# Order of the first mixer's projections, and the counting of split weights, in a two-network kernel on one core

## The chip, the cores and the metric

The kernel runs on one NeuronCore of one Trainium2 chip. The core has TensorE (PE; its weight loads are listed apart as PEld), VectorE (DVE), ScalarE (ACT), GpSimd (POOL) and SyncE (SP), each with its own queue, and sixteen DMA engines. SP's queue issues nearly all loads. The metric is the device time of one launch in microseconds (us), the median of several runs.

## The reference

Two two-layer networks are run one after the other on 256 tokens of width 1024, in float32. The first network has a bidirectional gated DeltaNet mixer (with pooling), a short convolution mixer, and an expert-choice feed-forward with 16 experts behind each; the second has an RG-LRU/SSD layer and a stick-breaking attention layer. Only the first network's first mixer is touched. Cut to what matters:

```
proj = h @ w_in                          # for the latent stream and the context stream
q, k, v = silu(dw_conv(proj[qkv]))       # 4 heads of 128; q only for the latent stream
q, k = l2norm(q), l2norm(k)
t_mat = I + strict_lower(k k^T * decay) * beta     # per chunk of 64 tokens
u, wk = solve(t_mat, v * beta), solve(t_mat, k * beta * exp(gam))
for each chunk, forward and backward:    # context chunks first, then latent chunks
    w = u - wk s;  o = (q exp(gam)) s + (q k^T * decay) w;  s = decay_c s + k_dec^T w
y = [rms_norm(o) * silu(z), pooled] @ w_out
```

## The kernel before

Activations are kept feature-major. Weights come from HBM in chunks of 1 MB (128 x 2048 floats). A float32 product is made of three matmuls: each weight is split into a rounded high part `wh` (ScalarE copy, L209) and a rest `wl` (VectorE subtraction, L284), in parts of 128 x 512, and `ws()` (L321) issues high x high, high x low and low x high for each of 8 blocks. `weight()` (L270) hands out the split parts, in the order that was planned, and splits ahead into a ring of HBUFS = 6 buffers (tags h and l).

Chunks go through small rings: ring_a (2 buffers) for the adaLN weights, ring_b (2 buffers) for `ev_ws` (six chunks: K 0 and 1, V 2 and 3, Q 4 and 5; one chunk serves two heads), `ev_ts` (four, for Z) and `ev_out` (four). A load waits in SP's queue until its buffer is free. The expert weights (`wg`, `wu`, `wd`) use a ring of 12 in the memory that the mixer's tiles leave, and later also ring_a and ring_b.

The first mixer is a list of units, `ORDER["mixer0"]` (L35), that is traced in that order; the tile framework's scheduler then fixes each engine's queue when the kernel is built, from its own estimates, with the trace order as priority. So operations of later units do run ahead where the scheduler saw room. On the chip each queue runs in its fixed order. The units:

- K0 to K3, V0 to V3, Q0 to Q3: `project()` (L630). K and V make a context product of 24 matmuls (`qkvc`, PSUM tag b) and then a latent product of 24 (`qkv`, tag ps); Q has the latent one alone. The eviction is a three-tap convolution (`conv3`, L502: one ScalarE and two VectorE operations per half), Tanh, a VectorE product, and for K and V a transposition (`ktT`, tag a).
- G gates, W0 and W1 decay matrices, R0 to R3 `correlate()` (k k^T times decay, L676), with the diagonal blocks copied out by R2 and R3.
- D `diagonal()` (L714): inverts all 32 x 32 diagonal blocks at once on VectorE, 31 steps of a product and a subtraction (L724, L725) between block transposes; it ends with R and RT.
- I0 to I3, four parts each: `inverse()` (L732) builds the 128 x 128 inverses from the blocks by small products in `lv` (tag b).
- P0 to P3, two parts each: `step()` of the scan, forward and backward. C0 and C1 are the q k scores, U adds the shift to the latent stream in place, Z (four parts) are the gate and pooling projections `zp` (tag ps), A0 to A4 the remaining adaLN products (L424, eight chunks each).

PSUM tags have fixed banks: ps 2, ada 1, a 3, b 2. After the mixer come the pooling and the output norm, the product with `ev_out` (`residual()`), and the first expert layer.

Of the kernel before, what the change touches and what calls it, by code (L numbers as in the profile page):

```python
# [7 lines left out]
F32R = mybir.dt.float32r  # L8
# [5 lines left out]
P = 128  # L14
D = 1024
# [4 lines left out]
RING_A = 2  # L20
RING_B = 2
HBUFS = 6
HBUFS1 = 5
# [7 lines left out]
PART = 512  # L31


ORDER = {
# [139 lines left out]
class Kernel:  # L174
# [84 lines left out]

    def plan(self, pool, bufs, parts):  # L260

        self.hpool, self.hbufs, self.parts = pool, bufs, list(parts)

# [6 lines left out]
    def weight(self, key, i, h, ahead=None):  # L270

        k = (key, i, h)
        if k in self.parts:
            assert self.parts.index(k) <= 1
            self.parts = self.parts[self.parts.index(k):]
            for k_ in self.parts[:ahead or self.hbufs]:
                if k_ not in self.WS:
                    hl = [self.more_parts.get(k_, self.hpool).tile([P, PART], F32R, tag=n, name="w" + n) for n in "hl"]
                    self.WS[k_] = self.split(self.W[k_[0]][k_[1]][:, k_[2] * PART:(k_[2] + 1) * PART], *hl)
        return self.WS[k]  # L280
# [237 lines left out]
    def mixer0_parts(self):  # L518
        r = []
        for n in ORDER["mixer0"].split():  # L520
            if n[0] in "KVQ":
                r += self.ws_parts("ev_ws", [4 * "KVQ".index(n[0]) + int(n[1])])
            elif n == "Z":
                j = len([x for x in r if x[0] == "ev_ts"])
                r += self.ts_parts("ev_ts", range(2))[j:j + 4]
        return r

    def mixer0(self, xin, xp):

        nc, v, g = self.nc, self.nc.vector, self.nc.gpsimd  # L530
        tc = self.tc
# [4 lines left out]
        right = ExitStack()  # L536
        self.plan(right.enter_context(tc.tile_pool(name="hpool0", bufs=HBUFS, side="right")), HBUFS, self.mixer0_parts())
        hl_p = right.enter_context(tc.tile_pool(name="m0l", bufs=1, side="right"))
# [89 lines left out]
        rq = kp.tile([P, 2, 4], F32, name="rq")  # L628

        def project(part, h):  # L630

            n = 256 if part == 2 else 512
            segs = []
            if part < 2:
                segs.append(self.ps("qkvc", "b")[:, :256])
                self.ws(segs[0], "ev_ws", 4 * part + h, ctx)
            a = self.ps("qkv")
# [19 lines left out]
            b = self.ps("ktT", "a")  # L657
# [222 lines left out]
        units = {"G": gates, "W0": each(decays(0), 4), "W1": each(decays(1), 4), "U": whole, "D": invert, "C0": lambda: scores(0), "C1": lambda: scores(1), "Z": each(zpool(), 4)}  # L880
        for h in range(4):
            units[f"K{h}"] = lambda h=h: project(0, h)
            units[f"R{h}"] = lambda h=h: cor(h)
            units[f"V{h}"] = lambda h=h: project(1, h)
            units[f"Q{h}"] = lambda h=h: project(2, h)
            units[f"I{h}"] = each(inverse(pairs[h]), 4)
            units[f"P{h}"] = each(steps(h), 2)
# [877 lines left out]
    def second(self):  # L1765
# [8 lines left out]
        with (self.tc.tile_pool(name="hpool2", bufs=HBUFS, side="right") as hpool,  # L1774
# [3 lines left out]
            self.chunks(parts)  # L1778
            self.plan(hpool, HBUFS, [x for x in parts if x[0] != "e_gate"])
            h = pr.tile([P, KT, T2], F32, name="h2")  # L1780
# [122 lines left out]
```

## Time and profile before

| | us |
|---|---|
| median of 3 runs | 1262.93 |
| lowest and highest | 1258.85, 1270.01 |
| profiled execution, its own time | 1264.06 |
| its span in the profile | 1262.3 |

| engine | busy us | share of the span |
|---|---|---|
| PE | 1102.4 | 87% |
| PEld | 752.2 | 60% |
| DVE | 635.5 | 50% |
| ACT | 492.8 | 39% |
| POOL | 68.0 | 5% |

Times in the rows below are from the span's start. Busy time counts the engine's own instructions; the ends of matmuls are modelled. PEclk is the granted TensorE clock as a share of full speed. DMA share is the mean busy share of the sixteen DMA engines. In rows of groups, "x16" is the number of instructions, then come the busy time, the mean length of one in ns, and the idle time in front of them with what ended it. In this kernel a line such as L209, L230 or L284 is that of a helper, and the tile names tell the use. A fp32 matmul on plain float32 data is recorded as two instructions.

### The profile page before, as it was taken

The page shows a single profiled execution, that of the slowest core. Times are in us where ns is not written, and L with a number is a line of the kernel's source. Part 1 is how long each engine was busy: PE and PEld are TensorE (multiplying, and loading weights), DVE is VectorE, ACT ScalarE, POOL GpSimd, SP SyncE. Part 2 cuts the span into 40 slices and gives each one's busy share as a digit, 9 for nine tenths or more (in the row PEclk, how much of TensorE's full clock was granted, in tenths as well). Part 3 has the DMA queues.
Part 4 walks back from the last instruction along what each step waited for, and adds up shares of the span by engine and source line. Part 5 has one row for each costly group of instructions (what it writes and reads, how often), then busy time and mean ns, then how long its engine had stood idle before and what let it go on. Part 6 is the DMA issues. An engine that isn't in the chain of part 4 may idle for free.

```text
span 1262.3 us, 19466 instructions
## 1 busy us (share of the span) xinstructions
PE 1102.4 (87%) x7728; PEld 752.2 (60%) x7728; DVE 635.5 (50%) x1442; ACT 492.8 (39%) x1035; POOL 68.0 (5%) x118
## 2 busy tenths in 40 slices
PE   5999699998799776699979967668999999999997
PEld 2667367767544211189954421116898699988875
DVE  3448854634421100178731110016887888689875
ACT  4346254424211000165521100005788465566663
POOL 0050000000000000000000000000001100011100
PEclk9899689999799867899979987778999999999999
DMA  9578655457999999999459999995252135433220
GB/s 387 198 278 319 235 201 201 138 214 310 401 421 420 421 421 422 422 420 383 167 224 383 421 421 422 421 422 218 102 199 101 67 139 185 165 134 130 101 101 34
DMA packets 48043, 339.71 MB, mean 269 GB/s; under 512 B 5328, under 2 KB 5584, under 8 KB 7248
## 3 DMA queue, kind: packets, MB, share of 16 engines
q1 hardware_dynamic: 46800, 336.38, 67.4%
q10 hardware_dynamic: 1152, 2.09, 0.5%
q8 instruction: 61, 1.00, 0.3%
q14 instruction: 30, 0.25, 0.1%
HBM read 337.40 MB, written 1.05 MB: 268 GB/s over the span
## 4 chain that ended last, share of the span: by engine, by line
PE 54%; DMA 26%; issue 7%; DVE 7%; ACT 4%; POOL 2%; POOLq 0%; SPq 0%; DVEq 0%; ACTq 0%
DMA w<-wu 8%; DMA w<-wd 8%; DMA w<-wg 7%; PE gu L1100 3%; PE ada L424 3%; PE xg L1075 2%; PE qkvg L329 2%; PE qkvg L331 2%; PE sc L329 2%; PE sc L330 2%; PE sc L331 2%; PE qkvg L330 2%; DMA w<-sc_in 1%; PE res L330 1%; PE res L329 1%
## 5 line engine op out<-in xcount | busy, mean ns | idle before, releaser
L284 DVE TENSOR_TENSOR wl<-w,wh 128x512 fp32r<-128x512 f32 x304 | 209.1, 696 | 83.3 <-ACT wh L209 79.2
L209 ACT ACTIVATE wh<-w 128x512 fp32r<-128x512 f32 x304 | 188.8, 629 | 154.5 <-PE res L330 27.2
L1100 PE MATMUL gu<-w,xg 128*32 128x512 f32 x1024 | 158.3, 721 | 46.6 <-DMA w<-wu 27.0
L1100 PEld LDWEIGHTS gu<-w,xg 128*32 128x32 f32 x1024 | 30.7, 118 | 158.1 <-DMA w<-wu 74.0
L1126 PE MATMUL dn<-w,hidT 128*32 128x512 f32 x512 | 74.5, 686 | 21.0 <-DMA w<-wd 15.1
L230 DVE SCALAR_TENSOR_TENSOR xT<-sc,adac,xT 128x256 f32<-128x256 f32 x64 | 27.9, 479 | 111.1 <-PE sc L1134 111.1
L209 ACT ACTIVATE y<-dn 128x512 f32<-128x512 f32 x16 | 9.6, 597 | 189.9 <-PE dn L1126 189.9
L1115 DVE TENSOR_TENSOR hid<-hid,gu 128x512 f32<-128x512 f32 x8 | 5.5, 685 | 153.8 <-PE gu L1100 153.8
L329 PE MATMUL qkvg<-u_f,wh 128*128 128x272 f32 (+1 forms) x256 | 74.3, 290 | 0.0
L331 PE MATMUL qkvg<-u_f,wl 128*128 128x272 f32 (+1 forms) x256 | 73.2, 286 | 0.0
L330 PE MATMUL qkvg<-u_f,wh 128*128 128x272 f32 (+1 forms) x256 | 72.8, 284 | 0.0
L424 PE MATMUL ada<-w,cs 128*32 128x512 f32 x320 | 51.1, 650 | 7.2 <-DMA w<-ada 7.2
L331 PE MATMUL sc<-hT,wl 128*128 128x258 f32 x192 | 54.5, 284 | 0.9 <-DVE wl L284 0.9
L1126 PEld LDWEIGHTS dn<-w,hidT 128*32 128x32 f32 x512 | 14.6, 118 | 68.2 <-DMA w<-wd 38.3
L329 PE MATMUL sc<-hT,wh 128*128 128x258 f32 x192 | 54.7, 285 | 0.2 <-ACT hT L289 0.2
L330 PE MATMUL sc<-hT,wh 128*128 128x258 f32 x192 | 54.3, 283 | 0.0
L329 PEld LDWEIGHTS qkvg<-u_f,wh 128*128 128x128 f32 x256 | 48.2, 188 | 3.1 <-issue 2.0
L331 PEld LDWEIGHTS qkvg<-u_f,wl 128*128 128x128 f32 x256 | 48.3, 189 | 0.8 <-issue 0.8
L330 PEld LDWEIGHTS qkvg<-u_f,wh 128*128 128x128 f32 x256 | 48.2, 188 | 0.0
L1134 PE MATMUL sc<-sg,y 128*128 128x256 f32 x128 | 40.2, 469 | 8.3 <-ACT y L209 8.3
L1134 PEld LDWEIGHTS sc<-sg,y 128*128 128x128 f32 x128 | 28.5, 234 | 26.8 <-ACT y L209 22.3
L1114 ACT ACTIVATE hid<-gu 128x512 f32<-128x512 f32 x8 | 4.8, 597 | 100.5 <-PE gu L1100 100.5
(613 smaller groups left out, 2642.5 us busy)
## 6 DMA issues: line engine op xcount, KB each, us to landing
w<-wu SPq DMA_DIRECT2D x64, 1024.0 KB, 19.8
w<-wg SPq DMA_DIRECT2D x64, 1024.0 KB, 19.8
w<-wd SPq DMA_DIRECT2D x64, 1024.0 KB, 19.8
w<-ada SPq DMA_DIRECT2D x48, 1024.0 KB, 5.0
w<-f_in SPq DMA_DIRECT2D x16, 1024.0 KB, 4.8
w<-sc_in SPq DMA_DIRECT2D x12, 1024.0 KB, 20.7
w<-e_out SPq DMA_DIRECT2D x8, 1024.0 KB, 5.4
w<-ev_ws SPq DMA_DIRECT2D x6, 1024.0 KB, 6.0
```

Of the source, the lines that this page charges most:

```text
L209: return self.nc.scalar.activation(out, in_, AF.Copy)
L230: return self.nc.vector.scalar_tensor_tensor(out, a, s, b, op0=op0, op1=op1, **kw)
L284: self.nc.vector.tensor_sub(lo, x, hi.bitcast(F32))
L329: mm(out, wh, xh, start=(kt == 0), stop=False)
L330: mm(out, wh, xl, start=False, stop=False)
L331: self.last_mm = mm(out, wl, xh, start=False, stop=(kt == nk - 1)).ins
L424: nc.tensor.matmul(a[32 * q:32 * q + 32, :], self.cs[:, kt, :], w[:, q * 512:(q + 1) * 512], start=(kt == 0), stop=(kt == KT - 1), tile_po ...
L1075: nc.tensor.matmul(a[:, :256], xn[:, i, ft * P:(ft + 1) * P], oh[:, i].rearrange("p e s -> p (e s)"), start=(i == 0), stop=(i == 1))
L1100: nc.tensor.matmul(a[32 * e:32 * e + 32, :], xg[g // 2][:, kt, s:s + 32], w[:, e * 512:(e + 1) * 512], start=(kt == 0), stop=(kt == KT - 1 ...
L1115: v.tensor_mul(hid, hid, pu[1])
L1126: nc.tensor.matmul(a[32 * e:32 * e + 32, :], hT[:, t, 32 * e:32 * e + 32], w[:, e * 512:(e + 1) * 512], start=(t == 0), stop=(t == 3), til ...
L1134: nc.tensor.matmul(a[:, j * 256:(j + 1) * 256], y[:, (2 * f2 + j) * P:(2 * f2 + j + 1) * P], sg[g // 2][:, g % 2], start=True, stop=True)
```

## The change

The mixer's order is rewritten: all K, then Q0, R0 to R3, all V (V3 ahead of V2) and Q1 to Q3 stand ahead of D; A2 and A3 stand behind it, U ahead of P0, and C0 and the four parts of each I are placed anew. The context product of K and V becomes a unit of its own (k0 to k3, v0 to v3), which leaves its bank in `first` for project(). The mixer's ring of split parts has 7 buffers instead of 6. `weight()` now counts the uses that each part has left (8 for a K or V part, 4 by default, 1 or 2 for the token-major ones) and splits the next part into a buffer when the part in it has none left, so a part may be asked for again after later ones.

```diff
@@ -19,6 +19,7 @@
 T2 = 272
 RING_A = 2
 RING_B = 2
+HBUFS0 = 7
 HBUFS = 6
 HBUFS1 = 5
 EARLY = 1, 2
@@ -32,8 +33,9 @@
 
 
 ORDER = {
-    "mixer0": "K0 G A0 W0 A1 W1 W0 W1 W1 W1 W0 W0 K1 R0 K2 A2 K3 R1 A3 R2 R3 V0 D V1 I0 V2 I0 V3 I1 Q0 I0 Q1 I0 I1 "
-          "Q2 I1 P0 P0 I3 P1 I1 Q3 C0 U P1 I2 Z I2 C1 P2 Z Z I2 I3 I2 P3 P2 A4 I3 Z I3 P3",
+    "mixer0": "k0 K0 G A0 W0 A1 W1 W0 W1 W1 W1 W0 W0 k1 K1 k2 K2 k3 K3 Q0 R0 R1 R2 R3 v0 V0 v1 V1 v3 V3 v2 V2 Q1 Q2 "
+              "Q3 D A2 A3 I0 I0 I1 I0 I0 I1 U I1 P0 I2 I3 P1 I1 P0 P1 C0 Z I2 C1 P2 Z Z I2 I3 P3 I2 P2 A4 I3 Z I3 "
+              "P3",
     "e": "L0 L1 U L3 L6 L2 L5 L7 L4 X9 X10 G2 G3 G4 G0 G6 G1 G7 X11 G5 X7 X6 X0 X2 X1 X5 X8 X4 Z1 X3 Z7 DT T "
           "Z3 S R Z0 R S S S Z2 R Z4 R H S S M Z6 O5 H Z5 O6 O3 O0 O1 H O7 N0 O2 H O4 N1",
     "f": "J1 J0 J3 J2 J4 B0 J5 J6 J7 B0 B0 B1 J8 J10 J9 B1 J11 B1 B2 J12 J13 J15 B2 J14 B3 B2 J19 J16 J17 B3 "
@@ -257,9 +259,13 @@
         self.nc.sync.dma_start(t, src)
         self.W.setdefault(key, {})[i if i is not None else len(self.W[key])] = t
 
-    def plan(self, pool, bufs, parts):
-
-        self.hpool, self.hbufs, self.parts = pool, bufs, list(parts)
+    def plan(self, pool, bufs, parts, uses=None):
+
+
+        self.hpool, self.hbufs, self.parts, self.nsplit = pool, bufs, list(parts), 0
+        self.left = {k: (uses or {}).get(k, 1 if k[0] in self.TS else 4) for k in self.parts}
+
+    TS = "ev_ts", "f_out"
 
     def ws_parts(self, key, ms, nk=KT):
         return [(key, i // 16, i % 16 // 4) for m in ms for i in range(m * nk, m * nk + nk, 4)]
@@ -270,13 +276,20 @@
     def weight(self, key, i, h, ahead=None):
 
         k = (key, i, h)
-        if k in self.parts:
-            assert self.parts.index(k) <= 1
-            self.parts = self.parts[self.parts.index(k):]
-            for k_ in self.parts[:ahead or self.hbufs]:
-                if k_ not in self.WS:
-                    hl = [self.more_parts.get(k_, self.hpool).tile([P, PART], F32R, tag=n, name="w" + n) for n in "hl"]
-                    self.WS[k_] = self.split(self.W[k_[0]][k_[1]][:, k_[2] * PART:(k_[2] + 1) * PART], *hl)
+        at = self.parts.index(k)
+        while self.nsplit < min(len(self.parts), at + (ahead or self.hbufs)):
+            k_ = self.parts[self.nsplit]
+            pool = self.more_parts.get(k_, self.hpool)
+            if pool is self.hpool:
+                old = [x for x in self.parts[:self.nsplit] if x not in self.more_parts][-self.hbufs:]
+                if len(old) == self.hbufs and self.left[old[0]] > 0:
+                    break
+            hl = [pool.tile([P, PART], F32R, tag=n, name="w" + n) for n in "hl"]
+            self.WS[k_] = self.split(self.W[k_[0]][k_[1]][:, k_[2] * PART:(k_[2] + 1) * PART], *hl)
+            self.nsplit += 1
+        assert at < self.nsplit
+        if ahead is None:
+            self.left[k] -= 1
         return self.WS[k]
 
     def split(self, x, hi, lo, eng="act"):
@@ -518,8 +531,9 @@
     def mixer0_parts(self):
         r = []
         for n in ORDER["mixer0"].split():
-            if n[0] in "KVQ":
-                r += self.ws_parts("ev_ws", [4 * "KVQ".index(n[0]) + int(n[1])])
+            if n[0] in "kvKVQ":
+                p = self.ws_parts("ev_ws", [4 * "KVQ".index(n[0].upper()) + int(n[1])])
+                r += [x for x in p if x not in r]
             elif n == "Z":
                 j = len([x for x in r if x[0] == "ev_ts"])
                 r += self.ts_parts("ev_ts", range(2))[j:j + 4]
@@ -534,7 +548,8 @@
         keep = ExitStack()
         kp = keep.enter_context(tc.tile_pool(name="m0r", bufs=1, side="right"))
         right = ExitStack()
-        self.plan(right.enter_context(tc.tile_pool(name="hpool0", bufs=HBUFS, side="right")), HBUFS, self.mixer0_parts())
+        self.plan(right.enter_context(tc.tile_pool(name="hpool0", bufs=HBUFS0, side="right")), HBUFS0, self.mixer0_parts(),
+                  {k: 8 for k in self.ws_parts("ev_ws", range(8))})
         hl_p = right.enter_context(tc.tile_pool(name="m0l", bufs=1, side="right"))
         rc = ExitStack()
         self.pack_in("pkg", hl_p)
@@ -627,13 +642,18 @@
         rk = pr.tile([P, 4, 4], F32, name="rk")
         rq = kp.tile([P, 2, 4], F32, name="rq")
 
+        first = {}
+
+        def project_ctx(part, h):
+
+            a = self.ps("qkvc", "b")[:, :256]
+            self.ws(a, "ev_ws", 4 * part + h, ctx)
+            first[part, h] = a
+
         def project(part, h):
 
             n = 256 if part == 2 else 512
-            segs = []
-            if part < 2:
-                segs.append(self.ps("qkvc", "b")[:, :256])
-                self.ws(segs[0], "ev_ws", 4 * part + h, ctx)
+            segs = [first.pop((part, h))] if part < 2 else []
             a = self.ps("qkv")
             self.ws(a[:, :258], "ev_ws", 4 * part + h, lat)
             segs.insert(0, a[:, :256])
@@ -879,6 +899,8 @@
 
         units = {"G": gates, "W0": each(decays(0), 4), "W1": each(decays(1), 4), "U": whole, "D": invert, "C0": lambda: scores(0), "C1": lambda: scores(1), "Z": each(zpool(), 4)}
         for h in range(4):
+            units[f"k{h}"] = lambda h=h: project_ctx(0, h)
+            units[f"v{h}"] = lambda h=h: project_ctx(1, h)
             units[f"K{h}"] = lambda h=h: project(0, h)
             units[f"R{h}"] = lambda h=h: cor(h)
             units[f"V{h}"] = lambda h=h: project(1, h)
@@ -1776,7 +1798,7 @@
               self.tc.tile_pool(name="second", bufs=1) as pr):
             up = us.enter_context(self.tc.tile_pool(name="input", bufs=1, side="right"))
             self.chunks(parts)
-            self.plan(hpool, HBUFS, [x for x in parts if x[0] != "e_gate"])
+            self.plan(hpool, HBUFS, [x for x in parts if x[0] != "e_gate"], {k: 2 for k in self.ts_parts("f_out", [1])})
             h = pr.tile([P, KT, T2], F32, name="h2")
             self.layer_e(up, pr, h)
             self.dump("h1", h)
```

## Rows read from the trace of the kernel before

**Rows 1.** Engine time by stretch of the span; the first line names the columns.
```profile
core 0: us, PE busy (x) PEld busy (x) DVE busy (x) ACT busy (x) POOL busy (x), PEclk, DMA share, GB/s
...
99.00:132.70 33.70, 30.64 (x243) 22.60 (x243) 29.33 (x85) 19.62 (x56) 1.14 (x1) 1.00 0.79 282
132.70:148.50 15.80, 5.99 (x33) 0.72 (x33) 14.50 (x36) 1.94 (x6) 0.00 (x0) 0.65 0.90 348
148.50:162.50 14.00, 13.96 (x93) 10.46 (x94) 6.84 (x27) 7.87 (x25) 0.31 (x1) 0.54 0.23 76
162.50:200.00 37.50, 37.50 (x381) 27.41 (x382) 17.43 (x44) 19.40 (x54) 0.61 (x2) 0.95 0.68 244
200.00:277.00 77.00, 77.00 (x589) 55.11 (x586) 39.35 (x107) 31.14 (x82) 0.92 (x3) 1.00 0.48 167
...
345.00:572.00 227.00, 185.25 (x1178) 80.79 (x1178) 51.13 (x117) 37.65 (x71) 1.23 (x1) 0.86 1.01 421
```

**Rows 2.** Loads issued by SyncE's queue, 272 to 306 us: start, length, line, transfer, count.
```profile
272.20 4.28 SPq L257 DMA_DIRECT2D w<-wu  x2
285.51 0.33 SPq L257 DMA_DIRECT2D w<-wg  x1
...
303.67 2.08 SPq L257 DMA_DIRECT2D w<-wg  x4
```

**Rows 3.** Matmuls in order of time, 128 to 150 us; idle before in brackets.
```profile
128.64 0.29 PE L330 MATMUL qkv<-hl,wh 128*128 128x258 f32 x1
128.76 0.28 PE L331 MATMUL qkv<-hl,wl 128*128 128x258 f32 x1
...
132.69 1.06 PE L424 MATMUL ada<-w,cs 128*32 128x512 f32 x8
136.21 1.07 PE L424 MATMUL ada<-w,cs 128*32 128x512 f32 x8 [2.45 <-DMA w<-ada]
...
148.52 0.60 PE L754 MATMUL lv<-RT,A 32*32 32x32 f32 x8 [2.65 <-DVE RT L728]
149.05 0.58 PE L329 MATMUL qkvc<-hc,wh 128*128 128x256 f32 x1
```

**Rows 4.** ScalarE in order of time, 147 us.
```profile
147.13 1.90 ACT L209 ACTIVATE A<-R 32x128 f32<-32x128 f32 x6 [13.81 <-DVE R L727]
```

**Rows 5.** VectorE groups, 111.5 to 148.5 us: line, tiles, count, busy, mean ns, idle.
```profile
L725 DVE TENSOR_TENSOR ident<-ident,sub 128x31 f32<-128x31 f32 (+15 forms) x31 | 10.6, 341 | 0.8
L724 DVE TENSOR_TENSOR sub<-B,ident 128x31 f32<-128x31 f32 (+15 forms) x31 | 10.6, 341 | 0.7
L284 DVE TENSOR_TENSOR wl<-w,wh 128x512 fp32r<-128x512 f32 x6 | 4.1, 687 | 0.2 <-ACT wh L209 0.2
...
L230 DVE SCALAR_TENSOR_TENSOR cv<-sq,cv 128x512 f32<-128x512 f32 x2 | 1.4, 689 | 0.0
```

**Rows 6.** Matmul groups, 148.5 to 277 us.
```profile
L424 PE MATMUL ada<-w,cs 128*32 128x512 f32 x136 | 23.8, 658 | 0.0
...
L329 PE MATMUL qkv<-hl,wh 128*128 128x258 f32 x24 | 7.9, 329 | 0.0
...
L331 PE MATMUL qkvc<-hc,wl 128*128 128x256 f32 x16 | 6.1, 381 | 0.0
...
L653 PE MATMUL qkv<-ones,sq 128*128 128x1 f32 x16 | 2.2, 243 | 0.0
...
L202 PE MATMUL ktT<-ident,cv 128*128 128x128 f32 x8 | 1.7, 353 | 0.0
```

**Rows 7.** VectorE groups, 42 to 290 us.
```profile
L230 DVE SCALAR_TENSOR_TENSOR qT<-qkv,dnh,qT 128x255 f32<-128x255 f32 x8 | 3.8, 480 | 0.2
...
L230 DVE SCALAR_TENSOR_TENSOR lat<-hl,adac,hl 128x256 f32<-128x256 f32 x8 | 3.8, 478 | 0.1
...
L697 DVE TENSOR_TENSOR A<-kb,A 128x256 f32<-128x256 f32 x8 | 3.4, 424 | 0.1
L284 DVE TENSOR_TENSOR hl<-lat,hl 128x256 fp32r<-128x256 f32 x8 | 3.4, 422 | 1.0 <-ACT hl L209 1.0
```

## Prediction

> **What bounds the kernel now.** I read the stretches first. From 345 to 572 us the sixteen DMA engines are full (share 1.01) and TensorE waits on expert weights; in the mixer, 99 to 277 us, it is the other way round, TensorE is busy nearly everywhere and the DMA share is about half [rows 1]. The one hole in the mixer is 132.7 to 148.5 us: TensorE is busy 5.99 of 15.80 us, ScalarE 1.94, VectorE 14.50. The granted clock is 0.65 of full in it and 0.54 in the 14 us behind it, so most of that time lies at the lower of its two levels (1.2 instead of 2.4 GHz), and 0.95 up to 200 us [rows 1].
>
> Next, whether an earlier end of the mixer is worth its full length. SyncE's queue issues the first expert weight that needs the mixer's memory at 285.5 us, and the run of them at 303.7 us, after the last `ev_out` chunk [rows 2]. From there the DMA engines are full for over 200 us. So a microsecond taken from the mixer's end is a microsecond of the kernel, until something else holds those loads (a rival below).
>
> Then what TensorE waits for in the hole. In order of time it has only adaLN chunks, each when its load lands, and the hole ends with the first `lv` product of I0 on RT, the last result of the substitution D; the next matmul is a context product, `qkvc` [rows 3]. That order is the clue. `lv` and `qkvc` share PSUM tag b with two banks; before, I0 is traced ahead of V2, so V2's context product gets its bank behind I0's, and I0 waits for D. V2 and V3 have their latent halves done but can't be evicted, they hold split weights, and Q's eviction stands in ScalarE's queue behind the copy that waits 13.81 us for R [rows 4]. That banks go out in trace order is my reading of these rows, not a row.
>
> **The change part by part.** *Context products as units, and counted uses.* Each small unit stands right ahead of its large one (`v3 V3`), which is the order that project() had; the counting lets a part's buffer go after its last use, as the tile release does now. No instruction is added. I cost both at nothing. The seventh buffer lets a split start half a product earlier, about 12 x 0.12 us, hidden while TensorE has other products; from nothing to that gain.
>
> *V and Q ahead of D and I0.* This takes the wait for the bank away. What comes out of the time after 148.5 us: V2's and V3's context products, 48 matmuls, and three latent ones of Q, 72 matmuls (16 and 24 on each of three lines) [rows 6]. Their spacing at the full clock is 0.12 us [rows 3], so 5.8 + 8.6 us; with the transposes of V2 and V3 and the row sums of Q (busy 1.7 and 2.2 us, overlapping, I take 3) 17.4 us in all. They go into the hole.
>
> The price is on VectorE, which runs D without a pause in the second half of the hole [rows 4, 5]. D is 62 operations, 21.2 us busy [rows 5], and each eviction pushed in delays it by its own length. New ahead of D's end: V2's other half, 2 x 0.48 + 0.69; V3, 4 x 0.48 + 0.69; four Q at 3 x 0.48 (the third is shorter, I have its bound); four weight splits for Q2 and Q3 at 0.69 [rows 5, 7]. That is 1.7 + 2.6 + 5.8 + 2.8 = 12.8 us. R0 to R3 now follow all four K, so that up to three of them bunch ahead of D: between nothing and 3 x 4 x 0.42 = 5.1 us [rows 7], I take half, since R0's and R1's small operations can still run early. Left out of the sum, as it depends on the order that the scheduler picks: U (8 x (0.48 + 0.42) = 7.2 us) and the first seven splits for Z (4.8 us) could be put between D's steps too [rows 5, 7].
>
> So D ends at 148.5 + 12.8 + 2.5 = 163.8 us. From 132.7 us that is 31.1 us, in which TensorE has the 17.4 us and adaLN chunks, one per 3.52 us as they land, 1.07 us each [rows 3]: nine, 9.6 us. Idle: 31.1 - 27.0 = 4.1 us, against 9.8 now.
>
> *A2 and A3 behind D.* Their eight chunks each become the filler of last choice. The four that ran in the hole before and five more are in the sum above; 17 stood after it [rows 6], 12 would now. Ring a has two buffers, so SyncE's queue stands still behind an adaLN load while TensorE puts its chunk off; the ring b loads queued behind it (the `ev_ts` and `ev_out` chunks) then come late for Z. I cost that at nothing, with Z still 50 us away, and keep up to 5.3 us (five chunks not taken forward) for the range.
>
> *Ring b.* Q0 and Q1 share a chunk that now holds one of two buffers from Q0 to Q1, and V3 and V2 load into the other. Their chunk is wanted only after V0 and V1 (four products, 11.5 us at 24 x 0.12 each); I cost it at nothing, with one pace of 3.5 us as the other end.
>
> **The sum.** After D the old stretch is 128.5 us (148.5 to 277). Take away 14.0 x 0.46 + 37.5 x 0.05 = 8.3 us that the lower clock cost [rows 1], the 17.4 us moved and the five chunks moved, 5.3 us: 97.5 us. A hole of 4.1 us instead of 9.8 should leave some of the clock loss, 2 us. The mixer's matmuls end at 163.8 + 97.5 + 2 = 263.3 instead of 277, 13.7 us earlier; I take 13 for the small gaps that less filler leaves. The profiled execution took 1264.06 us (span 1262.3), 1.1 above the median of 1262.93 and inside its runs' 1258.85 to 1270.01: 1251 against itself, 1250 against the median.
>
> **Rivals.**
> 1. *The hole moves.* U and Z's splits do go between D's steps: D ends at 175.8 us, TensorE has 17.4 us and twelve chunks, 12.8 us, for 43.1 us, idle 13, and the clock falls as before. End 175.8 + 97.5 - 3.2 + 8.3 = 278.4: no gain, 1263. For it: VectorE already mixes foreign operations into D (six splits among its 62 steps [rows 5]). Against: the same U lets Z start, which fills. The same time comes out if the last adaLN loads set the end: two ring a buffers come free for expert weights only at 272 us [rows 2].
> 2. *Slower: the chain behind D, not TensorE, sets its length.* I0 to P3 is one chain of hand-offs between TensorE, ScalarE and VectorE. If the old 120.2 us (128.5 less the clock's 8.3) are that chain, taking filler out shortens nothing, and D's delay passes on whole: 163.8 + 120.2 = 284, 7 us late, up to 296 with D at 175.8; with D in the middle 290, 1276. It decides from a chain of 277 - 163.8 = 113 us. For it: four inverses and four scan pairs stand in series with nothing but Z, A4 and U beside them. Against: TensorE is busy 77.00 of 77 us at the end [rows 1], and the matmuls of the chain begin one after the other without idle time.
> The Trainium skill, Perfetto Trace Analysis, section Identifying the Most-Contended Engine, speaks for this rival: matmul busy time says little on how near TensorE is to its limit, weight-load busy time is the measure. By it the last stretch is loaded 55.11 of 77 us, 72%, so 28% would be waits, which less filler doesn't shorten. The trace has no gaps there, but the busy ends are modelled, so it doesn't refute it.
> 3. *The hole closes whole.* The idle 9.8, the clock's 8.3 and the 3.1 idle us of 99 to 132.7 [rows 1] all go: 21 us, 1242. For it: Z's 96 products could join. Against: D's delay.
>
> **How the numbers follow.** Forecast 0.50, with its own range 1242 to 1258; rival 3 0.14; rival 1 0.22; rival 2 0.14. A measurement of this kernel can tell about 1%, 12.6 us, so faster means below 1250.3. That takes a little over half of the forecast's chance (0.28) and rival 3: 0.42. Slower is rival 2, 0.14; the rest, 0.44, lies within 1%. The range goes from rival 3 with the gains left open (the earlier split, R's at nothing, some 4 us) to where rival 2 begins to weigh: 1238 to 1272.
>
> **What would show it.** Right: no idle stretch above 5 us on TensorE between 99 us and D's end; all `qkvc` products before the first `lv`; D's last operation near 164 us; granted clock above 0.9 behind it; the first expert load into the mixer's memory near 272 us instead of 285.5; everything behind moved by the same amount. Wrong: a hole of 10 us or more ahead of the first `lv` (rival 1), or small waits of TensorE on ScalarE and VectorE all through the scan with P3's end at or after 284 us (rival 2), or the expert loads not moved although P3 ends earlier.

## The result and the profile after

| | before | after |
|---|---|---|
| median, us (4 runs of each, same chip) | 1263.04 | 1248.61 |
| lowest and highest, us | 1258.85, 1270.01 | 1247.82, 1252.43 |
| profiled execution, us | 1264.06 | 1252.43 |
| its span, us | 1262.3 | 1250.7 |

The ratio after to before is 0.9884, 95% interval 0.9862 to 0.9906: faster by 14.4 us, with 13 forecast. The profiled execution of after is the slowest of its four, so the two profiles are only 11.6 us apart. Executions more than 1.5% above the fastest of their kernel are left out of the ratios: five of nine with U behind D, two of ten with D ahead of V, no others.

The stretches of the span of after, to be held against [rows 1]; the last two are moved to where the same work now lies:

```profile
core 0: us, PE busy (x) PEld busy (x) DVE busy (x) ACT busy (x) POOL busy (x), PEclk, DMA share, GB/s
99.00:132.70 33.70, 33.42 (x273) 28.18 (x272) 31.22 (x88) 25.64 (x72) 1.14 (x1) 1.00 0.69 248
132.70:148.50 15.80, 14.55 (x108) 11.48 (x106) 14.64 (x42) 10.45 (x25) 0.00 (x0) 1.00 0.60 215
148.50:162.50 14.00, 12.16 (x46) 5.82 (x46) 11.51 (x33) 3.85 (x9) 0.00 (x0) 0.63 0.68 232
162.50:200.00 37.50, 36.16 (x337) 22.75 (x337) 23.29 (x68) 20.07 (x57) 0.92 (x3) 0.95 0.73 273
200.00:265.00 65.00, 65.00 (x555) 42.40 (x549) 20.63 (x65) 19.54 (x63) 0.92 (x3) 1.00 0.52 176
331.00:558.00 227.00, 183.98 (x1156) 77.68 (x1156) 48.71 (x111) 36.38 (x69) 1.24 (x1) 0.86 1.01 418
```

Read the second row first: in the old hole TensorE is busy 14.55 of 15.80 us, where it was 5.99, and the clock is full instead of 0.65. The weight-load column says more than the busy one, 11.48 us against 0.72: these are products, not late adaLN chunks. In the third row a weaker stretch is left (the clock at 0.63), but it lies ahead of D's end and not behind it. The experts' stretch in the last row is what it was: full DMA engines for 227 us, 14 us earlier.

TensorE in order of time, idle before in brackets, against [rows 3]:

```profile
149.11 1.93 PE L437 MATMUL ada<-w,cs 128*32 128x512 f32 x8 [1.32 <-DMA w<-ada]
152.27 1.01 PE L673 MATMUL qkv<-ones,sq 128*128 128x1 f32 x4 [1.22 <-ACT sq L671]
153.21 1.93 PE L437 MATMUL ada<-w,cs 128*32 128x512 f32 x8
155.07 0.80 PE L353 MATMUL zp<-wh,hl 128*128 128x512 f32 x1
...
172.29 1.06 PE L437 MATMUL ada<-w,cs 128*32 128x512 f32 x8
174.54 0.51 PE L353 MATMUL zp<-wh,hl 128*128 128x512 f32 x1 [1.18 <-DVE zp L232]
...
175.88 0.43 PE L774 MATMUL lv<-RT,A 32*32 32x32 f32 x8
```

The longest idle time between 132 us and the first `lv` is 1.32 us. Before, there were four waits in the hole, of 2.45, 4.20, 0.54 and 2.65 us, 9.8 in all; the longest, which [rows 3] leave out, was

```profile
141.47 1.93 PE L424 MATMUL ada<-w,cs 128*32 128x512 f32 x8 [4.20 <-DMA w<-ada]
```

The first `lv` comes at 175.88 us, 27.4 us later than before. What fills is new: from 155.07 us on `zp`, Z's products. By the order of TensorE's queue 51 of the 96 stand ahead of the first `lv`, and none did before; all eight context products of K and V stand ahead of it too.

VectorE at D's end, in order of time:

```profile
169.09 0.24 DVE L745 TENSOR_TENSOR ident<-ident,sub 128x87 f32<-128x87 f32 x1
169.25 0.42 DVE L297 TENSOR_TENSOR hl<-lat,hl 128x256 fp32r<-128x256 f32 x1
169.59 0.22 DVE L744 TENSOR_TENSOR sub<-B,ident 128x60 f32<-128x60 f32 x1
169.72 0.48 DVE L232 SCALAR_TENSOR_TENSOR lat<-hl,adac,hl 128x256 f32<-128x256 f32 x1
170.11 0.22 DVE L745 TENSOR_TENSOR ident<-ident,sub 128x60 f32<-128x60 f32 x1
170.24 0.69 DVE L297 TENSOR_TENSOR wl<-w,wh 128x512 fp32r<-128x512 f32 x1
...
171.99 1.98 DVE L747 STREAM_TRANSPOSE R<-ident 128x1024 f32<-128x1024 f32 x1
173.82 0.67 DVE L232 SCALAR_TENSOR_TENSOR zp<-zp 128x512 f32<-128x512 f32 x1
174.41 1.21 DVE L748 STREAM_TRANSPOSE RT<-R 128x1024 f32<-128x1024 f32 x1
```

Every second operation is foreign to D: U's `lat` and `hl` pairs, and the splits `wl` for Z. RT ends at 175.6 us. ScalarE's copy that waited 13.81 us for R [rows 4] waits no more:

```profile
174.13 1.90 ACT L211 ACTIVATE A<-R 32x128 f32<-32x128 f32 x6
```

SyncE's queue, against [rows 2]: the first `wg` load comes 10.8 us earlier, the run of four 13.4 us.

```profile
266.46 5.15 SPq L259 DMA_DIRECT2D w<-wu  x2
273.59 0.33 SPq L259 DMA_DIRECT2D w<-ev_out  x1
274.69 1.79 SPq L259 DMA_DIRECT2D w<-wg  x4
...
290.30 2.17 SPq L259 DMA_DIRECT2D w<-wg  x4
```

### The profile page after: what moved, and what is told of

Same layout as the page of the kernel before. It is cut to its first block, busy times and chain, and to the rows that moved or that the text cites. A ratio compares the mean times of both kernels' runs of the same rounds, so it can differ in the third digit from the quotient of the medians.

```text
span 1250.7 us, 19471 instructions
## 1 busy us (share of the span) xinstructions
PE 1094.5 (88%) x7728; PEld 741.0 (59%) x7728; DVE 629.2 (50%) x1442; ACT 492.8 (39%) x1035; POOL 68.6 (5%) x118
## 4 chain that ended last, share of the span: by engine, by line
PE 39%; DMA 23%; issue 7%; DVE 5%; ACT 2%; POOL 1%; POOLq 0%; DVEq 0%; SPq 0%; ACTq 0%
DMA w<-wu 8%; DMA w<-wg 8%; DMA w<-wd 6%; PE gu L1122 3%; PE xg L1097 2%; PE sc L344 2%; PE sc L342 2%; PE sc L343 2%; PE qkvg L342 2%; PE qkvg L344 2%; PE qkvg L343 2%; DMA pk<-pk 1%; PE dn L1148 1%; PE res L342 1%; PE res L343 1%
## 5 line engine op out<-in xcount | busy, mean ns | idle before, releaser
L1122 PE MATMUL gu<-w,xg 128*32 128x512 f32 x1024 | 161.0, 729 | 50.9 <-DMA w<-wu 28.1
L1148 PE MATMUL dn<-w,hidT 128*32 128x512 f32 x512 | 70.4, 652 | 21.7 <-DMA w<-wd 16.1
L437 PE MATMUL ada<-w,cs 128*32 128x512 f32 x320 | 54.6, 641 | 1.3 <-DMA w<-ada 1.3
L1156 PE MATMUL sc<-sg,y 128*128 128x256 f32 x128 | 37.3, 442 | 8.5 <-ACT y L211 8.4
```

The lines of the kernel that those rows point to most:

```text
L437: nc.tensor.matmul(a[32 * q:32 * q + 32, :], self.cs[:, kt, :], w[:, q * 512:(q + 1) * 512], start=(kt == 0), stop=(kt == KT - 1), tile_po ...
L1122: nc.tensor.matmul(a[32 * e:32 * e + 32, :], xg[g // 2][:, kt, s:s + 32], w[:, e * 512:(e + 1) * 512], start=(kt == 0), stop=(kt == KT - 1 ...
L1148: nc.tensor.matmul(a[32 * e:32 * e + 32, :], hT[:, t, 32 * e:32 * e + 32], w[:, e * 512:(e + 1) * 512], start=(t == 0), stop=(t == 3), til ...
L1156: nc.tensor.matmul(a[:, j * 256:(j + 1) * 256], y[:, (2 * f2 + j) * P:(2 * f2 + j + 1) * P], sg[g // 2][:, g % 2], start=True, stop=True)
```

## The experiments

Theory 1 is the prediction's: V2's and V3's context products stood behind I0 for a bank of tag b, in trace order; with V ahead, TensorE works while VectorE inverts, and the mixer ends earlier by the TensorE time that is no longer lost. Rivals: it is not the order but the number of banks; it is Q, or the adaLN chunks, or the seventh buffer; the chain of hand-offs behind D sets the end and TensorE's volume does not. Ratios are to the kernel before, run beside each on the same chip.

**V ahead of the first I0, nothing else** (in the kernel before; D, A2, A3, Q and R at their old places):

```diff
-    "mixer0": "K0 G A0 W0 A1 W1 W0 W1 W1 W1 W0 W0 K1 R0 K2 A2 K3 R1 A3 R2 R3 V0 D V1 I0 V2 I0 V3 I1 Q0 I0 Q1 I0 I1 "
+    "mixer0": "K0 G A0 W0 A1 W1 W0 W1 W1 W1 W0 W0 K1 R0 K2 A2 K3 R1 A3 R2 R3 V0 D V1 V2 V3 I0 I0 I1 Q0 I0 Q1 I0 I1 "
```

> Kernel before with one edit: V1, V2 and V3 traced ahead of I0, still behind D; Q, the six buffers, U, A2 and A3 stay where they were. Theory 1 (the two banks of tag b go out in trace order, and I0's product held the bank of V2's context product): the 48 context matmuls run ahead of the first lv product, the hole of 9.8 us shrinks to under 4 us, and at least two thirds of the change's 14 us come: 1248 to 1254 us. Rival (V and Q must stand ahead of D, or the seventh buffer and the counting do it): 1259 to 1266 us.

Measured: 1251.88 us, ratio 0.9905 (0.9873 to 0.9938). Two units, V2 and V3, moved ahead of the first I0 give some 12 of the 14.4 us. D stays ahead of them in the trace, so this is the order of V and I0 alone. In order of time:

```profile
157.83 0.28 PE L331 MATMUL qkv<-hl,wl 128*128 128x258 f32 x1
160.40 0.41 PE L754 MATMUL lv<-RT,A 32*32 32x32 f32 x8 [0.28 <-DVE RT L728]
```

The first line is the last of all the latent products. All 192 context products run ahead of the first `lv` now, and so do Q's 72 latent ones that stood behind it before, though nobody moved Q. TensorE is idle 4.1 us from 132 us to the first `lv`. None of U's operations and none of Z's products come ahead of D's end here, so D is less delayed than in the whole change, and with less to fill.

**The first I0 back ahead of V3 and V2** (in the kernel after; D moves ahead of them with it):

```diff
-    "mixer0": "k0 K0 G A0 W0 A1 W1 W0 W1 W1 W1 W0 W0 k1 K1 k2 K2 k3 K3 Q0 R0 R1 R2 R3 v0 V0 v1 V1 v3 V3 v2 V2 Q1 Q2 "
-              "Q3 D A2 A3 I0 I0 I1 I0 I0 I1 U I1 P0 I2 I3 P1 I1 P0 P1 C0 Z I2 C1 P2 Z Z I2 I3 P3 I2 P2 A4 I3 Z I3 "
+    "mixer0": "k0 K0 G A0 W0 A1 W1 W0 W1 W1 W1 W0 W0 k1 K1 k2 K2 k3 K3 Q0 R0 R1 R2 R3 v0 V0 v1 V1 D I0 v3 V3 v2 V2 Q1 Q2 "
+              "Q3 A2 A3 I0 I1 I0 I0 I1 U I1 P0 I2 I3 P1 I1 P0 P1 C0 Z I2 C1 P2 Z Z I2 I3 P3 I2 P2 A4 I3 Z I3 "
```

> Changed kernel with one edit: D and the first part of I0 traced ahead of V3 and V2, the rest as changed. Theory 1: the context products of V3 and V2 wait for the first lv product again, TensorE is idle 8 us or more ahead of it, and the time goes back to 1257 to 1266 us. Rival (the order of the banks doesn't matter, the rest of the new order brings the gain): 1247 to 1252 us.

Measured: 1256.51 us, ratio 0.9935 (0.9913 to 0.9958), just under what was expected. TensorE in order of time is the picture of [rows 3] again:

```profile
139.47 1.63 PE L437 MATMUL ada<-w,cs 128*32 128x512 f32 x8 [4.16 <-DMA w<-ada]
...
152.86 0.60 PE L774 MATMUL lv<-RT,A 32*32 32x32 f32 x8 [2.04 <-DVE RT L748]
153.39 0.58 PE L342 MATMUL qkvc<-hc,wh 128*128 128x256 f32 x1
```

The context product comes half a microsecond behind the first `lv`, with no wait of its own. Some 7 of the 14.4 us are lost again. The time alone doesn't say to what, since D's move ahead of V costs as much by itself (D ahead of V, below); what I0's place does is seen in the order: with I0 ahead, 48 context products stand behind the first `lv`; with D alone ahead, none.

**Three banks instead of two** (in the kernel before):

```diff
-    BANKS = {"ps": 2, "ada": 1, "a": 3, "b": 2}
+    BANKS = {"ps": 2, "ada": 1, "a": 2, "b": 3}
```

> Kernel before with three banks in tag b and two in tag a, order unchanged. Theory 1 in its strict form (a tag's banks are given out in trace order, so V2's context product stands behind I0's product whatever their number): the context products of V2 and V3 still run behind the first lv product, the hole of 8 to 12 us stays, and the time is 1260 us or more. Rival (two banks are simply too few): all eight context products run ahead of lv and 5 us or more are gained.

Measured: 1267.65 us, ratio 1.0021 (1.0000 to 1.0042). In order of time:

```profile
145.14 1.93 PE L424 MATMUL ada<-w,cs 128*32 128x512 f32 x8 [5.24 <-DMA w<-ada]
150.81 0.60 PE L754 MATMUL lv<-RT,A 32*32 32x32 f32 x8 [3.74 <-DVE RT L728]
151.35 0.58 PE L329 MATMUL qkvc<-hc,wh 128*128 128x256 f32 x1
```

A third bank gains nothing: `lv` still stands ahead of `qkvc`, with the same 48 context products behind it. They run between I0's own products (the next `lv` comes at 153.94 us), so a bank was free for them. The order is the cause, not the number of banks; the price of the bank taken from tag a is in this time too. That it is the order within tag b, the kernel before shows: nine units' latent products (216, in tag ps) ran ahead of its first `lv`, three units more than are traced ahead of I0, and only the context products waited.

**Q1 to Q3 traced behind D again** (in the kernel after):

```diff
-    "mixer0": "k0 K0 G A0 W0 A1 W1 W0 W1 W1 W1 W0 W0 k1 K1 k2 K2 k3 K3 Q0 R0 R1 R2 R3 v0 V0 v1 V1 v3 V3 v2 V2 Q1 Q2 "
-              "Q3 D A2 A3 I0 I0 I1 I0 I0 I1 U I1 P0 I2 I3 P1 I1 P0 P1 C0 Z I2 C1 P2 Z Z I2 I3 P3 I2 P2 A4 I3 Z I3 "
+    "mixer0": "k0 K0 G A0 W0 A1 W1 W0 W1 W1 W1 W0 W0 k1 K1 k2 K2 k3 K3 Q0 R0 R1 R2 R3 v0 V0 v1 V1 v3 V3 v2 V2 "
+              "D A2 A3 I0 I0 I1 Q1 I0 I0 I1 Q2 Q3 U I1 P0 I2 I3 P1 I1 P0 P1 C0 Z I2 C1 P2 Z Z I2 I3 P3 I2 P2 A4 I3 Z I3 "
```

> Changed kernel with Q1 to Q3 traced behind D and among the parts of I0 and I1. Q uses no bank of tag b, so by theory 1 it runs ahead of the first lv product anyway and the time stays within 4 us of the changed kernel's: 1246 to 1253 us. Rival (placing Q ahead of D carries half of the gain): 1254 to 1259 us.

Measured: 1248.90 us, ratio 0.9874 (0.9837 to 0.9910), not to be told from the change. In order of time:

```profile
150.94 0.28 PE L344 MATMUL qkv<-hl,wl 128*128 128x258 f32 x1
167.08 0.43 PE L774 MATMUL lv<-RT,A 32*32 32x32 f32 x8
```

This is again the last latent product: Q uses no bank of tag b, and all of its products run ahead of the first `lv` wherever Q is traced. So Q needed no place ahead of D in the trace; the run doesn't show what Q behind D on the chip would cost. The scheduler did place U anew: three of its `lat` operations lie ahead of D's end instead of eight, 17 of Z's products ahead of the first `lv` instead of 51, and RT ends at 165.8 us.

**Six buffers for the split weights** (in the kernel after, `HBUFS0 = 6`):

> Changed kernel with six buffers for split weights instead of seven. The prediction put the seventh between nothing and 1.4 us: 1247 to 1253 us. Rival (the buffers carry a part of the gain, as the held weights of V2 and V3 filled four of six before): 1255 us or more.

Measured: 1250.83 us, ratio 0.9894 (0.9849 to 0.9940). The seventh buffer cannot be measured.

**A2 and A3 at their old places** (in the kernel after):

```diff
-    "mixer0": "k0 K0 G A0 W0 A1 W1 W0 W1 W1 W1 W0 W0 k1 K1 k2 K2 k3 K3 Q0 R0 R1 R2 R3 v0 V0 v1 V1 v3 V3 v2 V2 Q1 Q2 "
-              "Q3 D A2 A3 I0 I0 I1 I0 I0 I1 U I1 P0 I2 I3 P1 I1 P0 P1 C0 Z I2 C1 P2 Z Z I2 I3 P3 I2 P2 A4 I3 Z I3 "
+    "mixer0": "k0 K0 G A0 W0 A1 W1 W0 W1 W1 W1 W0 W0 k1 K1 k2 K2 A2 k3 K3 A3 Q0 R0 R1 R2 R3 v0 V0 v1 V1 v3 V3 v2 V2 Q1 Q2 "
+              "Q3 D I0 I0 I1 I0 I0 I1 U I1 P0 I2 I3 P1 I1 P0 P1 C0 Z I2 C1 P2 Z Z I2 I3 P3 I2 P2 A4 I3 Z I3 "
```

> The changed kernel with A2 and A3 at their old places, between the K products, instead of behind D. The prediction costed this move at nothing, up to 5.3 us. If it is nothing, 1246 to 1253, and TensorE as full as in the changed kernel from 132 to 178 us. If the late adaLN chunks are needed as filler ahead of D, the early ones are used up before it and TensorE idles over 5 us more there: 1253 to 1260. If ring a held the split weights' loads back, it is faster by 3 us or more: 1240 to 1246.

Measured: 1249.46 us, ratio 0.9898 (0.9868 to 0.9927): nothing, alone. Here four `lat` operations lie ahead of D's end, and 17 of Z's products ahead of the first `lv`.

**Both, Q behind D and A2, A3 early** (the two diffs above together):

> The changed kernel with both: Q1 to Q3 behind D, as before the change, and A2 and A3 at their old places, so that of the whole reordering only the context units, V ahead of D and the first I0, and R0 to R3 behind K3 are left. If V ahead of the first I0 is what the change lives from, 1246 to 1253 again, ratio 0.985 to 0.992. If it needs Q or the adaLN chunks as filler, TensorE idles over 5 us more from 132 to 178 us and it takes 1254 to 1260.

Measured: 1267.27 us (1258.40 to 1275.82), ratio 1.0027 (0.9994 to 1.0059). Neither the first expectation nor the second: not only is the gain gone, it is worse than the hole that was expected. Two moves that cost nothing one by one cost 18 us together. In the profiled execution, at the upper end of the runs, the stretches are (columns as above):

```profile
156.00:164.00 8.00, 4.54 (x32) 3.02 (x31) 7.04 (x25) 3.11 (x7) 0.00 (x0) 0.92 0.77 265
164.00:172.00 8.00, 4.85 (x40) 2.35 (x41) 6.88 (x20) 5.39 (x19) 0.00 (x0) 0.50 0.38 132
172.00:180.00 8.00, 8.00 (x52) 4.38 (x51) 3.08 (x11) 2.97 (x9) 0.31 (x1) 0.50 0.41 139
180.00:190.00 10.00, 10.00 (x77) 6.43 (x77) 3.94 (x9) 3.77 (x12) 0.00 (x0) 0.50 0.58 201
...
200.00:210.00 10.00, 10.00 (x71) 6.95 (x71) 3.27 (x9) 3.09 (x10) 0.00 (x0) 0.50 0.01 2
210.00:220.00 10.00, 10.00 (x96) 6.29 (x92) 1.69 (x6) 1.63 (x7) 0.00 (x0) 0.67 0.37 115
220.00:230.00 10.00, 10.00 (x51) 6.45 (x51) 1.62 (x4) 2.19 (x7) 0.30 (x1) 0.50 0.35 116
230.00:240.00 10.00, 9.92 (x77) 7.83 (x76) 5.12 (x14) 3.69 (x9) 0.31 (x1) 0.95 0.52 193
```

The hole, 156 to 172 us, is 6.6 us of idle time. But the clock is at its lower level until about 230 us but for a part of 210 to 220, with TensorE busy all the while. That is where most of the time went: 34.2 us are lost to the clock from 132 to 260 us, against 6.9 in the change (the table below). What made the hole is in TensorE's order:

```profile
167.97 0.63 PE L774 MATMUL lv<-RT,A 32*32 32x32 f32 x8
...
170.91 0.80 PE L353 MATMUL zp<-wh,hl 128*128 128x512 f32 x1 [0.33 <-ACT hl L211]
```

Z's first product comes behind the first `lv`. All of V's and Q's products still run ahead of it, and eight adaLN chunks from 130 us on, as many as in the change. What is missing ahead of D's end is U and with it Z: eight `lat` operations and 51 products in the change, three or four and 17 with either move alone, none with both. That alone doesn't make the loss: V ahead of I0 alone has none there either, but its D ends at 160.3 us and 4.1 us are idle ahead of the first `lv`; here D ends at 167.3 us and 8.4 are idle. Why D ends later here was not tried apart.

**The same kernel once more**, to see whether the clock makes its spread:

> The kernel with Q1 to Q3 behind D and A2, A3 early once more, for one look at another execution: its runs lay 17 us apart, the profiled one at the upper end, with 43.7 us of TensorE lost from 132 to 260 us (9.5 idle, 34.2 to a granted clock below full). If the clock makes the spread, this execution's idle time is again 9 to 10 us, and its time differs from 1275.8 by about as much as its loss to the clock differs from 34.2 us. If something else does, the loss to the clock is again near 34 us whatever the time.

Measured, one execution: 1268.18 us, 9.7 us idle from 132 to 260 us and 25.5 us lost to the clock. So 7.6 us less time with 8.7 us less lost to the clock and the same idle time: as far as two executions can show it, the spread of this kernel is the clock.

**U behind D** (in the kernel after; the eight `lat` operations wait until D's transpose to R, the last but one, is issued, and with them Z):

```diff
-            v.transpose(mat(R).rearrange("p n c -> p c n"), X)
+            self.d_end = v.transpose(mat(R).rearrange("p n c -> p c n"), X).ins
...
-                self.stt(t, hi.bitcast(F32), self.adac[0][:, ft:ft + 1], lo.bitcast(F32), OP.add, OP.add)
+                with tc.issue_after(self.d_end):
+                    self.stt(t, hi.bitcast(F32), self.adac[0][:, ft:ft + 1], lo.bitcast(F32), OP.add, OP.add)
```

> Changed kernel with U's VectorE work held behind D's last step, so that Z can't start while D runs. D should then end near 164 us, as the prediction had it, instead of 175.6. Theory 2 (D is later by U's and Z's own length, but Z's products fill TensorE, so both cancel): the hole comes back, 6 us or more idle ahead of the first lv product, and the time is 1249 to 1256 us. Rival (the prediction's sum: adaLN chunks fill enough, and an earlier D is a gain): 1243 to 1248 us.

Measured: ratio 0.9943 (0.9887 to 0.9999), with three executions at 1252.05 to 1253.00 us and the other six at 1269.65 to 1280.84. VectorE at D's end, in order of time:

```profile
162.30 1.91 DVE L747 STREAM_TRANSPOSE R<-ident 128x1024 f32<-128x1024 f32 x1
164.07 0.41 DVE L232 SCALAR_TENSOR_TENSOR lat<-hl,adac,hl 128x256 f32<-128x256 f32 x1
164.40 1.23 DVE L748 STREAM_TRANSPOSE RT<-R 128x1024 f32<-128x1024 f32 x1
```

The stretch ahead of it, with the columns of the stretches above:

```profile
148.00:162.00 14.00, 7.16 (x37) 1.40 (x36) 12.55 (x39) 1.89 (x4) 0.00 (x0) 0.80 0.83 291
```

Without U and most of Z's splits D ends at 165.6 us, 10 us earlier than in the change. Yet nothing is gained, in the best executions either: TensorE is idle 6.84 us of these 14, since Z can't fill (2 of its products stand ahead of the first `lv`). What U takes from D it gives to TensorE.

**D traced ahead of V** (in the kernel after, V still ahead of I0):

```diff
-    "mixer0": "k0 K0 G A0 W0 A1 W1 W0 W1 W1 W1 W0 W0 k1 K1 k2 K2 k3 K3 Q0 R0 R1 R2 R3 v0 V0 v1 V1 v3 V3 v2 V2 Q1 Q2 "
-              "Q3 D A2 A3 I0 I0 I1 I0 I0 I1 U I1 P0 I2 I3 P1 I1 P0 P1 C0 Z I2 C1 P2 Z Z I2 I3 P3 I2 P2 A4 I3 Z I3 "
+    "mixer0": "k0 K0 G A0 W0 A1 W1 W0 W1 W1 W1 W0 W0 k1 K1 k2 K2 k3 K3 Q0 R0 R1 R2 R3 D v0 V0 v1 V1 v3 V3 v2 V2 Q1 Q2 "
+              "Q3 A2 A3 I0 I0 I1 I0 I0 I1 U I1 P0 I2 I3 P1 I1 P0 P1 C0 Z I2 C1 P2 Z Z I2 I3 P3 I2 P2 A4 I3 Z I3 "
```

> Changed kernel with D traced ahead of V and Q, which stay ahead of I0. By theory 1 the context products run ahead of lv as before this edit, and D, now first in line, ends earlier, 160 to 168 us; what D gains, TensorE loses in fillers, so the time stays within 5 us of the changed kernel's: 1245 to 1254 us. Rival (D's end sets the rest): 10 us of earlier D give 1238 to 1243 us.

Measured: 1258.40 us (1250.59 to 1273.98), ratio 0.9948 (0.9918 to 0.9978), a miss on the high side. The first `lv` is at 163.2 us, 12.7 us earlier than in the change, but TensorE is idle 6.3 us from 148 to 162 and the clock is 0.68 behind it. All context products run ahead of the first `lv` here too, and one of Z's.

**Z's products left out** (in the kernel after; copies of weight tiles stand in for the gate and pooling projections, so 96 products are missing):

```diff
-                self.ts(aa, lat, "ev_ts", part, range(0, 4))
...
+                    v.tensor_copy((zt if part == 0 else pt)[:, i], self.W["ev_ts"][2 * part + 1][:, i * 512:i * 512 + 512])
```

> Changed kernel without the products of Z: the gate and pooling projections are left out, and copies of weight tiles stand in their place, so its output is not the reference's. In the changed kernel the time from the first lv product to the scan's last product is 97.2 us, and 45 of Z's 96 products lie in it, some 10.6 us. Theory 3 (TensorE's volume sets that stretch): it falls to 85 to 90 us. Rival (the chain of hand-offs sets it, and Z is only filler): 94 to 98 us. Ahead of the first lv product the hole should come back, 8 us or more, since nothing fills D's second half.

Measured, one execution: 1255.69 us, first `lv` at 177.7, last scan product at 272.2 us, so 94.5 us. That is in the chain's band, but the clock is not the same: TensorE is idle 18.3 us from 132 to 260 us and the clock loses 20.8. Behind the first `lv` alone it loses 9.6 us here (0.73 up to 200 us, 0.94 up to 260) and 1.7 in the change (0.93 up to 200 us). Without these losses the stretch would be some 85 against 95.5 us, an estimate: 10.6 less, which is what Z's 45 products in it take. 96 products fewer bring the scan's end forward by only 0.9 us, as 51 of them lay ahead of D's end, the first `lv` comes 1.8 us later, and the clock takes 7.9 us more behind it.

**96 more products behind D** (in the kernel after), the other way round. The first half of the pooling projection is run five times, each pass starting the sum anew; `last` closes the sum of a pass, and the code for that is cut:

```diff
...
-                self.ts(aa, lat, "ev_ts", part, range(0, 4))
+                for last in (False,) if part == 0 else (True,) * 4 + (False,):
+                    self.ts(aa, lat, "ev_ts", part, range(0, 4), last)
```

> The changed kernel with 96 extra products: the first half of the pooling projection (Z's second pair of outputs) is run five times into the same banks, each pass starting the sum anew, so the output is the same. All of the extra ones lie behind D, in the stretch from the first lv to the last scan product, which took 97.2 us. At the spacing of Z's products, some 0.235 us, they are 22.6 us of TensorE. If TensorE's volume sets that stretch, the last scan product comes 18 to 23 us later, 291 to 296 us instead of 273.1, and the time is 1267 to 1272. If the chain of hand-offs sets it, the extra products go into its waits: at most 6 us later, 1249 to 1255. In between, each has a share by proportion.

Measured: 1268.52 us, ratio 1.0041 (1.0025 to 1.0057), 19.9 us above the change for 22.6 us of products, inside the band of TensorE's volume. In the profiles the last scan product is 13.8 us later (286.9 us), below that band. TensorE's groups from 175 to 286.9 us show the added products, 142 where the change has 46 behind its first `lv`:

```profile
L355 PE MATMUL zp<-wh,hl 128*128 128x512 f32 x48 | 19.7, 411 | 0.0
L354 PE MATMUL zp<-wl,hl 128*128 128x512 f32 x47 | 19.4, 413 | 0.0
L353 PE MATMUL zp<-wh,hl 128*128 128x512 f32 x47 | 19.2, 412 | 0.0
```

And SyncE's loads of `wg`, 14.0 and 15.3 us behind those of the change:

```profile
288.66 1.81 SPq L259 DMA_DIRECT2D w<-wg  x4
...
305.64 2.08 SPq L259 DMA_DIRECT2D w<-wg  x4
```

The 13.8 us understate it: this profiled execution is the fastest of its ten, the change's the slowest of its four. The stretch behind the first `lv` grew by 14.5 us (97.2 to 111.7), and the change lost 1.7 us to the clock in it, this kernel none: 16.2 of 22.6 us. By the medians it is 19.9. So the stretch behind D is set by TensorE's volume in the main, and waits swallow some 3 to 6 us of the 22.6.

**All runs together.** One measure orders them: the TensorE time lost from 132 to 260 us, as idle time plus each stretch's length times one less its granted clock, summed over 132, 148, 162, 178, 200 and 260 us. (Idle time at a low clock counts twice, and a loss ahead of D's end need not delay what follows, as 5.2 of the 6.9 us of the change from 148 to 162 us; so it is rough.) Each line is one profiled execution; only kernels with the same work are listed.

| kernel | idle, us | lost to the clock, us | both, us | time, us |
|---|---|---|---|---|
| Q behind D | 5.3 | 5.0 | 10.3 | 1245.95 |
| after | 4.4 | 6.9 | 11.4 | 1252.43 |
| six buffers | 4.7 | 6.9 | 11.7 | 1252.36 |
| A2, A3 early | 7.0 | 7.0 | 14.0 | 1252.58 |
| U behind D | 9.8 | 8.4 | 18.1 | 1253.00 |
| V ahead of I0 alone | 6.6 | 15.3 | 21.8 | 1258.35 |
| D ahead of V | 8.2 | 13.6 | 21.8 | 1258.31 |
| I0 ahead of V3, V2 | 11.5 | 12.0 | 23.5 | 1256.12 |
| before | 9.8 | 13.7 | 23.5 | 1264.06 |
| three banks | 10.7 | 18.8 | 29.6 | 1268.17 |
| Q behind D, A2, A3 early, again | 9.7 | 25.5 | 35.2 | 1268.18 |
| Q behind D, A2, A3 early | 9.5 | 34.2 | 43.7 | 1275.82 |

From end to end 33.4 us lost go with 29.9 us of time. The idle time alone orders them badly (9.5 to 10.7 us stand beside 1253 and 1276); the clock's share does most of the ordering. Lines next to each other differ by up to 8 us for other reasons that the runs don't name.

## Why the prediction was right, and the step that failed

- *The cause of the hole* (tag b's banks go out in trace order, `lv` ahead of `qkvc`): right, and now shown: V2 and V3 moved alone give 12 us, a third bank gives none, and products in other banks pass I0 in the queue. I0 put back brings the old order and 10.1 us of idle time back, but its 7 us may as well be D's move ahead of V.
- *Context units, counted uses, the seventh buffer at nothing*: the buffer holds. The units and the counting were not tried alone; nor was R behind K3. But V ahead of I0 gives its 12 us without any of them.
- *Q ahead of D*: the sum had 8.6 us of Q's products among the 17.4 us that go into the hole. They do go there, but not for their place in the trace: once V stands ahead of I0, they run ahead of the first `lv` with Q traced on either side of D.
- *A2 and A3 at nothing*: their old places cost nothing by themselves, but 18 us with Q traced behind D as well, where the scheduler puts neither U nor Z ahead of D's end; the bound of 5.3 us was too narrow for that, as it left out U, Z and the clock. The chunks' own term was too large: the sum takes five chunks, 5.3 us, out of the stretch behind D, 12 instead of 17, and has nine in the hole by 163.8 us. In the change six have started by then, and 16 stand behind the first `lv` (128 instructions, where [rows 6] have 136), so the term is worth 1.1 us:

```profile
L437 PE MATMUL ada<-w,cs 128*32 128x512 f32 x128 | 25.2, 633 | 0.0
```

- *D's end at 163.8 us*: this step failed. RT ends at 175.6 us, 11.8 later and within 0.2 us of rival 1's 175.8. The text left U and Z's splits out "as it depends on the order that the scheduler picks"; the scheduler put them between D's steps one by one. With U held back D ends at 165.6 us, so the rest of that sum (evictions, splits, R) was sized right to 2 us.
- *Why the time came out all the same*: the same operations let Z start. Its 51 products ahead of the first `lv` are 51 x 0.235 = 12.0 us of TensorE work that the forecast had behind D. So the delay was 27.4 us instead of 15.3 (12.1 more), and the stretch from the first `lv` to the last scan product shrank from 135.3 us (148.5 to 283.8) to 97.2 (175.9 to 273.1), 38.1 us where 128.5 - 99.5 = 29.0 were forecast (9.1 more). Of these 9.1, Z gives 12.0 and the missing adaLN chunks take 4.2; the last 1.3 are not assigned. Two errors of one source nearly cancel, which is luck in this sum: rival 1's delay came together with rival 3's filler. The text named both ("the same U lets Z start, which fills"), but kept them as two cases, when they are one. That the sum's own case would have done nearly as well, V ahead of I0 alone shows: without U in D, D ends at 160.3 us, 4.1 us are idle, as forecast, and some 12 us are gained.
- *Rival 2* (a chain of at least 113 us behind D): refuted. The stretch is 97.2 us, and 16 to 20 of the 22.6 us of added products show. The Trainium skill, Perfetto Trace Analysis, section Identifying the Most-Contended Engine, names weight-load busy time, beside the share of peak that the matmuls reach, as the measure of TensorE's headroom. The prediction's step from it, that a weight-load share of 72% leaves 28% of waits, doesn't hold here: in after the share is 0.65 from 200 to 265 us (42.40 of 65), and 22.6 us of added products still cost 19.9.
- *A microsecond of the mixer is one of the kernel*: right within 3 us. The scan's last product moved by 10.7 us, the `wg` loads by 10.8 and 13.4, the end of the span by 11.6. The 277 us that the text took for the end of the mixer's matmuls was too early: the scan's last product starts at 283.8 us before and at 273.1 after. The differences don't suffer, but "P3's end at or after 284 us" as a sign for rival 2 was where the kernel stood already.
- *The granted clock above 0.9 behind D*: right, 0.92 from 178 to 200 us and 1.00 behind. The forecast took 2 us for what the smaller hole leaves of the clock loss, and 1.7 are lost behind the first `lv`; the 0.63 of 148.5 to 162.5 us lies ahead of D's end, which VectorE sets.

A version that clearly beats the change wasn't found: Q behind D has 0.9874 to its 0.9884, within both intervals.

## What to carry to other kernels

Where two tiles share the banks of a tag, look at the order in which the trace asks for them: a product that could run may stand behind one that waits for another engine, and another bank doesn't help while the queue is in that order. An operation that is slipped into a chain on one engine is to be counted twice, as a delay of the chain and as what it releases elsewhere; leaving it out of both may give the right sum for the wrong reason. A unit's place in the trace is not its place in the queue: look at what moved on the engine before saying what a move cost. And two moves that are free one by one may let the scheduler place a third unit elsewhere: try them together before calling either free.

## What the runs showed of the hardware

The size of the clock's loss was not expected. In the kernel before, a hole with 9.8 us of idle time was followed by some 14 us at a mean of 0.54 and the clock was near full from then on [rows 1]. In the kernel with Q behind D and A2, A3 early, 9.5 us of idle time came with a granted clock of 0.50 (the lower of the two levels, 1.2 GHz) from 164 us on and for most of the 58 us from 172 to 230, though the profile has TensorE busy in every microsecond of these (the ends of matmuls are modelled); a second execution of it got back to 0.87 after 190 us, fell to 0.50 again from 210 to 220 us, and was 7.6 us faster. A profile that shows TensorE busy at 100% thus doesn't say that the clock comes back; only the clock's own column does. What decides when it comes back, the runs don't show.
